# A two-layer diffusion-transformer step on one core: splits of the next weights at fixed chunks and the next rows scaled ahead, in the second half of the in-projection's first quarter

## The chip, the cores and the metric

The kernel runs on one core of one Trainium2 chip. The metric is the device time of one execution in microseconds (us). The core has five engines that run side by side: TensorE (PE: matmuls; PEld: its weight loads), VectorE (DVE), ScalarE (ACT), GpSimd (POOL), and SyncE (SP), whose queue issues the DMAs. Each engine takes its instructions in order and waits on semaphores for what others must finish first.

## The reference, cut to what matters

Two groups of 128 tokens (a context pass and a denoising step) go through two layers with the same weights. Each layer modulates its normalised input with scale, shift and gate vectors that are themselves products of a condition vector with a large matrix, `w_ada`; the first thing that layer 0 does with the result is the in-projection.

```python
def rmsnorm(x, g):
    xf = x.astype(jnp.float32)
    y = xf * lax.rsqrt(jnp.mean(xf * xf, axis=-1, keepdims=True) + EPS)
    return (y * g.astype(jnp.float32)).astype(x.dtype)
...
        mod = jax.nn.silu(cond) @ w_ada[l] + b_ada[l]
        sh1, sc1, gt1, sh2, sc2, gt2 = jnp.split(mod[:, None, :], 6, axis=-1)
        h = rmsnorm(x, g_norm_mix[l]) * (1 + sc1) + sh1
...
    proj = h @ w_in
```

The inner size is D = 2048, that is 16 blocks of 128, called rows here; the in-projection has 23 output blocks of 128, called chunks. All inputs are fp32.

## The kernel before, in words

**A product in three.** Every fp32 product is made of three matmuls at reduced precision. An operand is split into a high part (a rounding to `F32R`) and a low part (what the rounding left). For each 128x128 block of weights, `gemm` issues high weights by high rows, high weights by low rows, and low weights by high rows. The weights arrive by DMA as raw tiles of 16 blocks (1 MB, three buffers, `raw`); `split` makes the high part `wh` on ScalarE (L245) and the low part `wl` on VectorE (L246), each in tiles of 8 blocks with four buffers. The rows live in `hx`: for row c, the high part stands in columns 0 to 255 and the low part in 256 to 511.

**The in-projection in quarters.** Since the shift and scale vectors of layer 0 must first be computed from `w_ada`, the in-projection does not wait for all of them: it runs over the 23 chunks several times, each time with only some of the 16 rows, and adds up (`part`). First with rows 0 and 1 (weights `whole`, copied out of PSUM by ScalarE), then with rows 2 and 3 (weights `halves`, added on VectorE, L1132), then with rows 4 to 7, 8 to 11 and 12 to 15 (weights `rest`). A chunk with two rows is 6 matmuls, one with four is 12. The three accumulator banks (`pacc`) are taken in turn, so a chunk waits for the sum of the third chunk before it.

**The steps between the chunks.** In each pass, steps written out by hand stand after certain chunks: `first_half`, `other_half` and, for the later passes, `quarter(q)` are tables from chunk number to step, which `part` calls through `between(c)`. A *unit* is a quarter of one of the vectors: unit (0, 1, 1) is the scale of rows 4 to 7, unit (0, 0, 1) their shift. `pair(u, t)` sums two tiles of `w_ada` for unit u on TensorE (`ada<-araw,condw`, `ada<-kv_in,condw`); after the second pair ScalarE copies the sum (`am`, L437). `turned` lets TensorE transpose that copy (L110) and VectorE reduce it and add the bias (L453, L455; for a scale also L462). `turned(1)` then calls `rows(1)`, which is `modulate`: for rows 4 to 7 VectorE multiplies x with the row factor `rb0` (L648) and with scale and shift for the first group of tokens (L654), ScalarE does so for the second (L657) and rounds to the high part (L658), and VectorE and GpSimd in turn make the low part (L643).

`scaled_rows` and `begin_row` do the same work in two steps, and are used for rows 0 to 3 before: the first makes x times factor times scale (L669, L672, VectorE), which needs no shift; the second adds the shift and splits: the high part on ScalarE (L681), the low part on VectorE (L682).

**Order.** The instructions that pass through `keep_order`, and all of TensorE's while `pe.in_turn` is set, stay in the order written. The others, the splits in `Weights.chunk` among them, are placed by a scheduler before the run, on each engine where they fit by its own reckoning. `Weights.ahead` splits half a raw tile at a fixed place (`pin`), in pieces of `FINE` = 4 blocks. `Feed` issues the loads of `w_ada` tiles and raw weights in one order, each as soon as its buffer is free; `feed.use` gives a buffer back.

The table that is changed reads, before:

```python
                other_half = {5: lambda: pair(2, 2), 7: turned, 13: lambda: pair(3, 0), 20: lambda: pair(3, 2),
                              22: lambda: turned(1)}
```

Of the kernel before, what the change touches and what calls it, by code (L numbers as in the profile page):

```python
# [12 lines left out]
AF = mybir.ActivationFunctionType  # L13
ALU = mybir.AluOpType
# [3 lines left out]
P = 128  # L18
# [43 lines left out]
FINE = 4  # L62
# [29 lines left out]
def step_kernel(ctx: ExitStack, tc: tile.TileContext, A: dict):  # L92
    nc = tc.nc
    dve, act, pool, sp = nc.vector, nc.scalar, nc.gpsimd, nc.sync
    kept = []

    def keep_order(i):
        if not any(i is j for j in kept):
            kept[:] = [i]
            tc.keep_in_program_order(i)  # L100
# [37 lines left out]
    def T_(pl, shape, tag, dt=F32, bufs=None):  # L138
        kw = {} if bufs is None else {"bufs": bufs}
        return pl.tile(shape, dt, tag=tag, name=nm(tag), **kw)  # L140
# [95 lines left out]
    def spread(r, bank=bank):  # L236

        ps = bank()
        for g in range(2):
            pe.matmul(ps[:, g * T:(g + 1) * T], r[:, g:g + 1].to_broadcast([P, P]), ident, start=True, stop=True)  # L240
        return ps[:, :NT]


    def split(out_hi, out_lo, src, pin=lambda i: i):
        pin(act.copy(out_hi, src))  # L245
        pin(dve.tensor_tensor(out=out_lo, in0=src, in1=out_hi.bitcast(F32), op=ALU.subtract))  # L246
# [3 lines left out]
    class Weights:  # L250
# [30 lines left out]
        def ahead(self, pin, mid=None):  # L281

            if not self.half:
                self.half = [self.take()[0], 0]
            raw, lo = self.half
            self.blocks += self.halves(raw, lo, pin, mid)
            self.half = None if lo else [raw, 8]
            if lo:
                self.used()

        def halves(self, raw, lo, pin=lambda i: i, mid=None):
            wh = T_(wpool, [P, 1024], "wh", F32R, bufs=4)
            wl = T_(wpool, [P, 1024], "wl", F32R, bufs=4)
            for at in range(0, 8, FINE):
                s = slice(at * P, (at + FINE) * P)
                split(wh[:, s], wl[:, s], raw[:, (lo + at) * P:(lo + at + FINE) * P], pin)
                if mid and at == 0:
                    mid()
            return [(wh[:, b * P:(b + 1) * P], wl[:, b * P:(b + 1) * P]) for b in range(8)]

        def chunk(self):
            while len(self.blocks) < self.nblk:
# [362 lines left out]
    def scaled_rows(rb, c0, n):  # L665
        nts = []
        for c in range(c0, c0 + n):
            h = T_(tmp, [P, NT], "nt", bufs=4)
            keep_order(dve.tensor_tensor(out=h, in0=x[:, c], in1=rb, op=ALU.mult))  # L669
            for g in range(2):  # L670
                s = slice(g * T, (g + 1) * T)
                keep_order(dve.tensor_scalar(out=h[:, s], in0=h[:, s], scalar1=scl[:, 0, 0, c, g:g + 1],  # L672
                                             scalar2=None, op0=ALU.mult))
            nts.append(h)
        return nts

    def begin_row(hx, h, c):
        for g in range(2):
            s = slice(g * T, (g + 1) * T)
            b_ = mod[:, 0, 0, c, g:g + 1]  # L680
            keep_order(act.activation(hx[:, c, s], h[:, s], AF.Identity, bias=b_))  # L681
            keep_order(dve.scalar_tensor_tensor(  # L682
                out=hx[:, c, NT + g * T:NT + (g + 1) * T], in0=h[:, s], scalar=b_,
                in1=hx[:, c, s].bitcast(F32), op0=ALU.add, op1=ALU.subtract))
# [40 lines left out]
    def operand(pl, tag):  # L725
        return home(pl, tag)[:, :KD * ROW].rearrange("p (k n) -> p k n", k=KD)
# [181 lines left out]
    def mixer_ab(hx, beside):  # L908
        l = 0
        with tc.tile_pool(name="ab", bufs=1) as ab:  # L910
            with tc.tile_pool(name="abp", bufs=1) as pj:
# [53 lines left out]
                def unit_pair(u, t):  # L965
                    for i in (t, t + 1):
                        sum_rows(i, feed.tiles.pop((*u, i)))
                    for i in (t, t + 1):
                        feed.use(("a", "s1", "a", "s3")[i])

                whole = Weights(A["w_in_ab"][0:3], 2, 8, cycle=23)
                halves = Weights(A["w_in_ab"][3:6], 2, 8, cycle=23)
                rest = Weights(A["w_in_ab"][6:], 4, 4, cycle=23)
                for w in (whole, halves, rest):
                    w.used = lambda: feed.use("raw")
# [15 lines left out]
                weights(whole)  # L991
                units(2, (0, 1))
                weights(halves)
                units(2, (2, 3))
                weights(halves)
                units(3, (0, 1))
                weights(halves)
# [26 lines left out]
                rb0 = spread(r)  # L1024
# [6 lines left out]
                def first_rows():  # L1031
                    unit.copy()
                    unit.turn()
                    for c in range(2):
                        begin_row(hx, nts[c], c)
# [103 lines left out]
                def rows(q):  # L1139
                    modulate(hx, rb0, 0, 0, range(4 * q, 4 * q + 4))  # L1140

                second = {}

                def half_begin(j):
                    second["u"] = HalfUnit(j, 1, ppool["first"], att_bank)
                    for t in range(2):
                        half_sums(second["u"], t)
                    second["u"].copy()

                def half_end(j):  # L1150
                    second["u"].turn()
                    if j == 0:
                        for i, h in enumerate(second["nt"]):
                            begin_row(hx, h, 2 + i)
# [4 lines left out]
                def pair(u, t):  # L1159
                    unit_pair(ROWS[u], t)  # L1160
                    if t == 2:
                        second["finish"] = ada_finish(*ROWS[u], False)
                        second["finish"].pop(0)()

                def turned(q=0):
                    second["finish"].pop(0)()
                    if q:
                        rows(q)

                first_half = {0: lambda: whole.ahead(keep_order), 4: lambda: half_begin(1), 6: lambda: half_end(1),  # L1170
                              10: stretch, 13: lambda: half_begin(0), 15: lambda: half_end(0), 22: lambda: pair(2, 0)}
                other_half = {5: lambda: pair(2, 2), 7: turned, 13: lambda: pair(3, 0), 20: lambda: pair(3, 2),
                              22: lambda: turned(1)}

                def quarter(q):
                    u = 2 * q + 2
# [345 lines left out]
    with banks("pab") as ppool["ada"]:  # L1522
        ppool["att"] = ppool["ada"]
        idle = T_(tmp, [P, 512], "am", bufs=1)
        keep_order(dve.memset(idle, 0.0))
        ps = T_(pacc, [P, 512], "acc")
        for _ in range(WARM):
            keep_order(pe.matmul(ps, idle[:, :P], idle, start=True, stop=True))
        for c in range(0, KD, 4):
            keep_order(sp.dma_start(out=x[:, c:c + 4], in_=A["xT"][:, c:c + 4]))  # L1530
        ppool["first"] = lambda: T_(ppool["ada"], [P, 512], "ada", bufs=1)
        hx = operand(keep, "hx")
        st = stat_init()
        with tc.tile_pool(name="beside", bufs=1) as beside:
            o = mixer_ab(hx, beside)
            with tc.tile_pool(name="raw", bufs=1) as rp:
                T_(rp, [P, SHIFT // 4], "pad")
                u = raw_tile(rp, "u")
                out_ab(o, st, u)
                W = Weights(A["w_up"][0], KD, 1)  # L1540
                hx, *begun = modulated(st, 0, 1, W, u, (keep, "hx"), rp)
# [22 lines left out]
    for c in range(KD):  # L1564
        if c in EARLY:
            pool.tensor_tensor(out=x[:, c], in0=x[:, c], in1=rbs, op=ALU.mult)
        else:
            dve.scalar_tensor_tensor(out=x[:, c], in0=x[:, c], scalar=C("gfin")[:, c:c + 1], in1=rb,  # L1568
                                     op0=ALU.mult, op1=ALU.mult)
# [136 lines left out]
```

## Time and profile before

| | |
|---|---|
| median of 3 runs | 2341.16 us (2339.91 to 2343.24) |
| the profiled execution, its own time | 2337.55 us |
| its span in the profile | 2335.8 us |
| TensorE busy, share of the span | 2304.0 us, 99% |
| VectorE, ScalarE, GpSimd busy | 1853.1, 1192.0, 179.7 us |
| moved by DMA | 612.98 MB, 262 GB/s in the mean |

The pass with rows 2 and 3 runs from about 50 to 75 us of the span; rows 4 to 7 begin after it. Busy times overlap, since the engines work side by side, and TensorE's is modelled: matmuls follow each other in a pipeline, so the distance from one start to the next says more than a length. In an answer in order of time the columns are start, length, engine, line, operation, output<-input, shapes, count, and in brackets the idle time ahead with what ended it. L107 is the line of every matmul, L110 of every transpose.

### The profile page before, as it was taken

The numbers are of one execution on the slowest core, as the hardware profiler recorded it, in microseconds if no ns is written. First come the engines' busy times: TensorE is split into PE (matmuls) and PEld (weight loads), VectorE is DVE, ScalarE is ACT, GpSimd is POOL, SyncE is SP. The second block draws the span as 40 slices with busy tenths as digits, with TensorE's granted clock in tenths as the row PEclk, the third lists the DMA queues.
The fourth block names the chain that finished last, engine by engine and source line by source line (L and its number), as shares of the span: only waits on it lengthen the run. The fifth ranks groups of instructions, "written<-read, shape, count | busy, mean of one in ns | idle before, by whom it ended". The sixth has DMA issues, their size and how long they took to land.

```text
span 2335.8 us, 47901 instructions
## 1 busy us (share of the span) xinstructions
PE 2304.0 (99%) x19692; PEld 2192.2 (94%) x19692; DVE 1853.1 (79%) x2864; ACT 1192.0 (51%) x1969; POOL 179.7 (8%) x240
## 2 busy tenths in 40 slices
PE   8899999999999999999999999999999999999998
PEld 6788768999999999999999999999999999999998
DVE  4669768889999999999978888798899755666654
ACT  4345545665554355555564544457655434555543
POOL 0001111310000000001130000023000000000011
PEclk9999999999999999999999999999999999999999
DMA  9887779677767777777778788677677555555553
GB/s 387 349 349 289 294 286 358 231 281 270 269 246 297 289 269 259 267 271 253 289 268 292 284 312 295 251 286 269 236 259 266 197 198 188 194 198 197 187 195 127
DMA packets 107099, 612.98 MB, mean 262 GB/s; under 512 B 11584, under 2 KB 19712, under 8 KB 39296
## 3 DMA queue, kind: packets, MB, share of 16 engines
q1 hardware_dynamic: 106880, 609.92, 70.9%
q8 instruction: 155, 2.54, 0.4%
q14 instruction: 64, 0.52, 0.1%
HBM read 605.12 MB, written 4.75 MB: 261 GB/s over the span
## 4 chain that ended last, share of the span: by engine, by line
PE 95%; DMA 2%; DVE 2%; ACT 1%; issue 0%; SPq 0%; POOL 0%; DVEq 0%; ACTq 0%; POOLq 0%
PE acc L107 87%; PE ada L107 4%; PE att L107 2%; DMA araw<-w_ada 1%; PE att L110 1%; DMA raw<-w_in_ab 1%; DVE wl L246 1%; PE misc L107 1%; PE ada L110 0%; DMA block<-w_ada 0%; DVE aacc L510 0%; ACT wh L245 0%; DVE x L1568 0%; SPq L956 0%; PE misc L110 0%
## 5 line engine op out<-in xcount | busy, mean ns | idle before, releaser
L107 PE MATMUL acc<-hx,wh 128*128 128x256 f32 (+1 forms) x7296 | 1261.4, 278 | 8.7 <-DVE hx L643 3.6
L245 ACT CAST wh<-raw 128x1024 fp32r<-128x1024 f32 (+2 forms) x824 | 796.3, 976 | 917.7 <-PE acc L107 777.2
L246 DVE TENSOR_TENSOR wl<-raw,wh 128x1024 fp32r<-128x1024 f32 (+2 forms) x824 | 920.0, 1132 | 280.4 <-ACT wh L245 275.3
L107 PEld LDWEIGHTS acc<-hx,wh 128*128 128x128 f32 x7296 | 1103.8, 188 | 31.8 <-issue 11.7
L107 PE MATMUL acc<-hx,wl 128*128 128x256 f32 (+1 forms) x3648 | 1010.3, 277 | 2.8 <-DVE wl L246 2.8
L107 PEld LDWEIGHTS acc<-hx,wl 128*128 128x128 f32 x3648 | 686.5, 188 | 4.5 <-DVE wl L246 3.6
L107 PE MATMUL acc<-g,wh 128*128 128x256 f32 x2816 | 478.9, 276 | 0.0
L107 PEld LDWEIGHTS acc<-g,wh 128*128 128x128 f32 x2816 | 423.7, 188 | 0.0
L107 PE MATMUL acc<-g,wl 128*128 128x256 f32 x1408 | 388.2, 276 | 0.0
L107 PE MATMUL acc<-hxc,wh 128*128 128x256 f32 (+1 forms) x1536 | 277.4, 282 | 0.0
L481 DVE CUSTOM_DVE_ANT_0 junk<-araw,condb 128x2048 f32<-128x2048 f32 x120 | 275.7, 2298 | 0.0
L107 PEld LDWEIGHTS acc<-g,wl 128*128 128x128 f32 x1408 | 264.2, 188 | 0.0
L107 PEld LDWEIGHTS acc<-hxc,wh 128*128 128x128 f32 x1536 | 236.3, 188 | 8.7 <-issue 8.4
L107 PE MATMUL acc<-hxc,wl 128*128 128x256 f32 (+1 forms) x768 | 213.8, 278 | 0.0
L510 DVE SCALAR_TENSOR_TENSOR aacc<-block,condw,aacc 128x512 f32<-128x512 f32 x240 | 171.8, 754 | 28.4 <-DMA block<-w_ada 28.1
L208 POOL TENSOR_TENSOR sqacc<-sqacc,sq 128x256 f32<-128x256 f32 x62 | 72.0, 1161 | 1514.1 <-ACT sq L204 1508.0
L107 PEld LDWEIGHTS acc<-hxc,wl 128*128 128x128 f32 x768 | 144.7, 188 | 0.3
L1461 ACT ACTIVATE cv<-acc,convw 128x256 f32<-128x256 f32 x170 | 94.9, 559 | 0.0
L107 PE MATMUL ada<-araw,condw 128*32 128x512 f32 (+1 forms) x704 | 89.6, 592 | 3.0 <-DMA araw<-w_ada 3.0
L838 DVE SCALAR_TENSOR_TENSOR x<-acc,mod,x 128x128 f32<-128x128 f32 x190 | 57.3, 342 | 34.6 <-PE acc L107 34.5
L1467 DVE SCALAR_TENSOR_TENSOR cv<-acc,convw,cv 128x254 f32<-128x254 f32 x170 | 81.3, 478 | 3.3
L1464 DVE SCALAR_TENSOR_TENSOR cv<-acc,convw,cv 128x254 f32<-128x254 f32 x170 | 80.6, 474 | 0.0
(250 smaller groups left out, 1414.2 us busy)
## 6 DMA issues: line engine op xcount, KB each, us to landing
raw<-w_up SPq DMA_DIRECT2D x176, 1024.0 KB, 4.8
araw<-w_ada SPq DMA_DIRECT2D x144, 1024.0 KB, 5.7
raw<-w_down SPq DMA_DIRECT2D x88, 1024.0 KB, 4.8
raw<-w_in_c SPq DMA_DIRECT2D x48, 1024.0 KB, 5.9
block<-w_ada SPq DMA_DIRECT2D x128, 256.0 KB, 5.7
raw<-w_in_ab SPq DMA_DIRECT2D x18, 1024.0 KB, 9.8
raw<-w_out_ab SPq DMA_DIRECT2D x16, 1024.0 KB, 8.6
raw<-w_out_c SPq DMA_DIRECT2D x16, 1024.0 KB, 6.8
```

Of the source, the lines that this page charges most:

```text
L107: return self.placed(nc.tensor.matmul(*a, **kw))
L110: return self.placed(nc.tensor.transpose(*a, **kw))
L208: eng.tensor_tensor(out=st["acc"], in0=st["acc"], in1=sq, op=ALU.add)
L245: pin(act.copy(out_hi, src))
L246: pin(dve.tensor_tensor(out=out_lo, in0=src, in1=out_hi.bitcast(F32), op=ALU.subtract))
L481: keep_order(dve.tensor_tensor_reduce(out=T_(feat["pool"], [P, D], "junk"), in1=feat["row"][:, c], in0=feat["raw"].rearrange("p g n -> p ( ...
L510: i = dve.scalar_tensor_tensor(out=acc[c], in0=block, scalar=condw[:, k, c:c + 1], in1=acc[c], op0=ALU.mult, op1=ALU.add)
L838: dve.scalar_tensor_tensor(out=x[:, c, s], in0=ps[:, s], scalar=mod[:, l, 3 * which + 2, c, g:g + 1], in1=x[:, c, s], op0=ALU.mult, op1=AL ...
L1461: pin(act.activation(y, ps, AF.Identity, scale=cw[:, 1, m:m + 1], bias=cw[:, 3, m:m + 1]))
L1464: pin(dve.scalar_tensor_tensor(out=y3[:, :, 1:], in0=p3[:, :, :T - 1], scalar=cw[:, 0, m:m + 1], in1=y3[:, :, 1:], op0=ALU.mult, op1=ALU.add))
L1467: pin(dve.scalar_tensor_tensor(out=y3[:, :, :T - 1], in0=p3[:, :, 1:], scalar=cw[:, 2, m:m + 1], in1=y3[:, :, :T - 1], op0=ALU.mult, op1=A ...
```

## The change

Three things change in the pass with rows 2 and 3. The splits of raw tiles, those of `halves` and of the first tile of `rest`, are put at fixed places (after chunks 7, 8, 14, 15, 18 and 20), half a tile each, in pieces of four blocks; before, the scheduler placed them, mostly in pieces of eight. For that `ahead` and `halves` learn to take a tile that is not full. Rows 4 to 7 are made by `scaled_rows` after chunk 10 and `begin_row` after chunk 19 in place of `modulate` after chunk 22; for rows 5 and 7 the high part of the second group of tokens is made on VectorE (`both=False`), and GpSimd has no part in these rows. The pairs of unit (0, 0, 1) move from after chunks 13 and 20 to after 12 and 17, its turn from after 22 to after 19.

```diff
         def ahead(self, pin, mid=None):
 
             if not self.half:
-                self.half = [self.take()[0], 0]
-            raw, lo = self.half
-            self.blocks += self.halves(raw, lo, pin, mid)
-            self.half = None if lo else [raw, 8]
+                self.half = [*self.take(), 0]
+            raw, n, lo = self.half
+            self.blocks += self.halves(raw, lo, pin, mid, min(8, n - lo))
+            self.half = None if lo else [raw, n, 8]
             if lo:
                 self.used()
 
-        def halves(self, raw, lo, pin=lambda i: i, mid=None):
+        def halves(self, raw, lo, pin=lambda i: i, mid=None, n=8):
             wh = T_(wpool, [P, 1024], "wh", F32R, bufs=4)
             wl = T_(wpool, [P, 1024], "wl", F32R, bufs=4)
-            for at in range(0, 8, FINE):
-                s = slice(at * P, (at + FINE) * P)
-                split(wh[:, s], wl[:, s], raw[:, (lo + at) * P:(lo + at + FINE) * P], pin)
+            for at in range(0, n, FINE):
+                s = slice(at * P, min(at + FINE, n) * P)
+                split(wh[:, s], wl[:, s], raw[:, (lo + at) * P:min(lo + at + FINE, lo + n) * P], pin)
                 if mid and at == 0:
                     mid()
-            return [(wh[:, b * P:(b + 1) * P], wl[:, b * P:(b + 1) * P]) for b in range(8)]
+            return [(wh[:, b * P:(b + 1) * P], wl[:, b * P:(b + 1) * P]) for b in range(n)]
...
-    def begin_row(hx, h, c):
+    def begin_row(hx, h, c, both=True):
         for g in range(2):
             s = slice(g * T, (g + 1) * T)
             b_ = mod[:, 0, 0, c, g:g + 1]
-            keep_order(act.activation(hx[:, c, s], h[:, s], AF.Identity, bias=b_))
+            if g == 0 or both:
+                keep_order(act.activation(hx[:, c, s], h[:, s], AF.Identity, bias=b_))
+            else:
+                keep_order(dve.tensor_scalar(out=hx[:, c, s], in0=h[:, s], scalar1=b_, scalar2=None, op0=ALU.add))
             keep_order(dve.scalar_tensor_tensor(
...
-                other_half = {5: lambda: pair(2, 2), 7: turned, 13: lambda: pair(3, 0), 20: lambda: pair(3, 2),
-                              22: lambda: turned(1)}
+                def split_next(w):
+                    w.ahead(keep_order)
+
+                def four_scaled():
+                    second["nt"] = scaled_rows(rb0, 4, 4)
+
+                def four_rows():
+                    turned()
+                    for i, h in enumerate(second["nt"]):
+                        begin_row(hx, h, 4 + i, i % 2 == 0)
+
+                other_half = {5: lambda: pair(2, 2), 7: lambda: (turned(), split_next(halves)),
+                              8: lambda: split_next(halves), 10: four_scaled, 12: lambda: pair(3, 0),
+                              14: lambda: split_next(halves), 15: lambda: split_next(halves),
+                              17: lambda: pair(3, 2), 18: lambda: split_next(rest), 19: four_rows,
+                              20: lambda: split_next(rest)}
```

## The prediction

> **What bounds the kernel now.** I read the page's head first, then the busy times by stretch over the opening 200 us, then the order of instructions in time on TensorE and VectorE around the edit. The page gives the span and says that TensorE is the bound of the whole:
>
> ```profile
> span 2335.8 us, 47901 instructions
> PE 2304.0 (99%) x19692; PEld 2192.2 (94%) x19692; DVE 1853.1 (79%) x2864; ACT 1192.0 (51%) x1969; POOL 179.7 (8%) x240
> ```
>
> So an edit pays only where TensorE stands still or runs at a lower clock. The stretches show where that is; the columns are the stretch, its length, busy time (count) by engine, granted clock, DMA share, GB/s:
>
> ```profile
> 54.00:84.30 30.30, 22.51 (x174) 16.59 (x172) 20.18 (x41) 11.42 (x18) 3.40 (x2) 0.90 1.01 421
> 122.00:163.00 41.00, 41.00 (x350) 34.66 (x349) 26.94 (x51) 16.43 (x24) 1.64 (x2) 1.00 0.87 345
> 75.40:84.20 8.80, 2.82 (x13) 2.00 (x11) 8.35 (x16) 5.81 (x12) 3.40 (x2) 0.65 1.01 420
> 84.20:88.00 3.80, 3.71 (x17) 3.71 (x18) 1.12 (x4) 0.00 (x0) 0.00 (x0) 0.50 0.42 172
> ```
>
> The second half of the in-projection ends at 75.4 us. The next 8.8 us hold 2.82 us of matmuls and 8.35 us of VectorE work, and the 3.8 us after that run at a clock of 0.50. By 122 us there is no idle left. TensorE's own lines for this place (start, length, and in brackets the idle time and what ended it):
>
> ```profile
> 59.96 0.38 PE L107 MATMUL acc<-hx,wl 128*128 128x256 f32 x1 [0.98 <-DVE wl L246]
> 68.63 0.39 PE L107 MATMUL acc<-hx,wl 128*128 128x256 f32 x1 [0.74 <-DVE wl L246]
> 74.33 0.40 PE L107 MATMUL acc<-hx,wh 128*128 128x256 f32 x2
> 74.68 0.40 PE L107 MATMUL acc<-hx,wh 128*128 128x256 f32 x2
> 75.39 0.60 PE L110 MATMUL ada<-cst,am 128*128 128x128 f32 x4
> 78.45 0.58 PE L107 MATMUL acc<-hx,wh 128*128 128x256 f32 x1 [2.46 <-ACT hx L658]
> 80.11 0.58 PE L107 MATMUL acc<-hx,wh 128*128 128x256 f32 x1 [1.07 <-DVE hx L643]
> 84.29 0.58 PE L107 MATMUL acc<-hx,wh 128*128 128x256 f32 x1 [2.53 <-DVE hx L643]
> 84.89 0.63 PE L107 MATMUL acc<-hx,wh 128*128 128x256 f32 x2
> 85.53 0.63 PE L107 MATMUL acc<-hx,wh 128*128 128x256 f32 x2
> 88.08 0.46 PE L107 MATMUL acc<-hx,wh 128*128 128x256 f32 x2
> ```
>
> Three matmuls take 0.35 us at full clock (74.33 to 74.68), 0.117 each, and 0.64 us after the idle stretch (84.89 to 85.53), 0.213 each. Full pace is back at 88.08, with 24 matmuls of the next quarter done: 7 before 84.29 and 17 after it (the count of the 3.8 us stretch). At full clock 24 would take 2.8 us from the transposes' end near 75.8, that is until 78.6. So 88.1 - 78.6 = 9.5 us is the most that the turn of this unit can ever give back, 0.4% of the run. What ended the last wait is VectorE. Its queue through that stretch:
>
> ```profile
> 76.03 0.19 DVE L453 TENSOR_REDUCE mod<-ada 128x8 f32<-128x32 f32 x1
> 76.25 0.17 DVE L455 TENSOR_TENSOR mod<-mod,cst 128x8 f32<-128x8 f32 x1
> 76.34 1.22 DVE L246 TENSOR_TENSOR wl<-raw,wh 128x1024 fp32r<-128x1024 f32 x1
> 77.48 1.11 DVE L654 TENSOR_SCALAR nt<-nt,scl,mod 128x128 f32<-128x128 f32 x4
> 78.50 1.22 DVE L246 TENSOR_TENSOR wl<-raw,wh 128x1024 fp32r<-128x1024 f32 x1
> 79.64 0.42 DVE L643 TENSOR_TENSOR hx<-nt,hx 128x256 fp32r<-128x256 f32 x1
> 81.03 2.88 DVE L246 TENSOR_TENSOR wl<-raw,wh 128x1024 fp32r<-128x1024 f32 x2
> 83.83 0.41 DVE L643 TENSOR_TENSOR hx<-nt,hx 128x256 fp32r<-128x256 f32 x1
> 84.16 0.74 DVE L648 TENSOR_TENSOR nt<-x,misc 128x256 f32<-128x256 f32 x2
> ```
>
> The shift lands (76.03), four rows are made, and four weight remainders (wl, L246) stand between them, although only the first is needed at once. From the reduce to the last row's low part it is 84.24 - 76.03 = 8.2 us, nearly all of it VectorE at work.
>
> **The splits.** The number of elements split is the same; a split of 1024 becomes two of 512. One piece costs VectorE 0.68 busy, and the wide one overlaps its successor by 1.22 - (77.48 - 76.34) = 0.08; so 0.60 for a piece, 1.14 for the wide one. Two pieces cost 0.06 more than one wide split, ten pieces or so 0.3 in all, beside matmuls except where they are named below.
>
> ```profile
> L246 DVE TENSOR_TENSOR wl<-raw,wh 128x512 fp32r<-128x512 f32 x4 | 2.7, 683 | 0.0
> L682 DVE SCALAR_TENSOR_TENSOR hx<-nt,mod,hx 128x128 fp32r<-128x128 f32 x4 | 1.3, 349 | 0.5 <-ACT hx L681 0.5
> L672 DVE TENSOR_SCALAR nt<-nt,scl 128x128 f32<-128x128 f32 x4 | 1.0, 282 | 0.0
> L681 ACT ACTIVATE hx<-nt,mod 128x128 fp32r<-128x128 f32 x4 | 1.3, 394 | 0.0
> 64.23 1.85 PE ada L107 x16
> ```
>
> At chunk 7 the split now stands behind the unit's three small VectorE steps (0.31 for the first two, by 76.03 to 76.34, and 0.2 for the third), but its first piece is shorter by 0.54. Chunk 8's wait of 0.98 therefore stays as it is. At chunk 16 the wait of 0.74 ended with a wide split; with a piece it ends 0.4 earlier. I take 0.4.
>
> **The scaled rows** at chunk 10: per row one product of 0.33 and two of 0.20 (0.282 less the overlap), 2.9 us for four. VectorE has room for them: 20.18 us busy in the 30.3 us stretch, and a pair of 1.85 us on TensorE follows at chunk 12. If that cover were missing, an accumulator would come free late, 0.4 us at most by the order of the queue. I take nothing.
>
> **The pairs** move from chunks 13 and 20 to 12 and 17, past no other load on SP's queue; only the moment changes at which two buffers come free. The second pair needs its last tile:
>
> ```profile
> 56.76 0.64 SPq L942 DMA_DIRECT2D kv_in<-w_ada  x1
> kv_in<-w_ada SPq DMA_DIRECT2D x1, 1024.0 KB, 10.6
> 57.46 4.04 SPq L271 DMA_DIRECT2D raw<-w_in_ab  x2
> raw<-w_in_ab SPq DMA_DIRECT2D x1, 1024.0 KB, 11.2
> ```
>
> It is issued at 56.76 and lands 10.6 later, at 67.4. TensorE reaches the end of chunk 17 near 69.6 (the 72.9 of the next part, less two chunks and a pair): covered by 2 us. The two weight tiles with which the next quarter begins are issued at 57.5 and 61.2, and the second lands 11.2 later, at 72.4: ahead of the splits that chunk 18 now asks for and of those behind them. The DMA engines are full in this stretch (1.01), so an earlier issue brings nothing sooner.
>
> **The turn at chunk 19.** Three chunks of 0.70 fewer stand ahead of it, and 0.4 was saved: the transposes come at 75.39 - 2.1 - 0.4 = 72.9 rather than 75.39, so the reduce, 0.64 behind them as now (76.03), comes at 73.5. The built program's VectorE queue from there on, in order, is: reduce and bias (0.31); a piece, an add of chunk 20, a piece, an add of 21; two low parts; an add of 22; a low part and a high part of row 5; a row product for the quarter after; two pieces; four low parts; a high part of row 7; a wide remainder of the second tile, a row product, another wide remainder, a row product; and only then the low part of row 7's second half, which the twelve matmuls of the next quarter's first chunk need. The wide remainders belong to chunks 4 to 7, yet stand ahead. The sum: 0.31 + 4 x 0.60 + 2 x 1.14 + three adds and three products of 128x256 at 0.33 (83.83 to 84.16) = 2.0 + eight low parts at 0.27 (0.349 less 0.08) = 2.2 + two high parts at 0.20 = 0.4: together 9.6 us. ScalarE's six high parts (0.32 apart, 2 us) and its splits run beside this. So the last row is ready at 73.5 + 9.6 = 83.1 against 84.24. The turn begins 2.5 us earlier, but VectorE has 1.4 us more to do before the last row, since the adds of three chunks and the low parts that GpSimd used to make now stand in this queue. Left: 1.1 us. TensorE then has 10 matmuls behind it (all nine of the first three rows and one of the fourth), not 7: 3 x 0.117 = 0.35 more. As the gaps are nearly as long as before, I take it that the cold 3.8 us follow the resumption again.
>
> **The rest.** From 163 to about 360 us, where the queues are not written out by hand, the scheduler places instructions anew; beyond that the order is the same. TensorE is without gaps there but for one place, the last heads:
>
> ```profile
> 331.70 0.30 PE L110 MATMUL att<-cst,p 128*128 128x128 f32 x1 [1.25 <-DVE p L895]
> 333.50 1.26 PE L107 MATMUL att<-pT,vm 128*128 128x128 f32 x6 [0.62 <-ACT pT L879]
> 334.70:338.40 3.70, 3.70 (x26) 1.30 (x26) 1.05 (x5) 1.63 (x6) 0.06 (x1) 0.64 0.00 0
> 331.84 0.82 PE L107 MATMUL att<-kg,qb 128*128 128x128 f32 x4
> 336.33 0.35 DVE L896 TENSOR_SCALAR p<-p,rec 128x256 f32<-128x256 f32 x1
> ```
>
> That place costs 1.25 + 0.62 + 0.36 x 3.7 = 3.2 us now. In the new order more output-projection matmuls stand ahead of the first of these waits, but the transposes of the next head then follow almost directly on its scores, and scores to weights takes 4.0 us (332.66 to 336.68). One gap closes, another opens; bounds: -3.2 (all gone) and +4.0 + 0.36 x 3.7 = +5.3 (a whole softmax uncovered, then cold). Lacking a row nearer to one, I take 0.
>
> **Sum.** 1.1 + 0.35 = 1.5 us off, within 0.5 and 2.5 for the size of VectorE's sum. The profiled execution took 2337.55 us, 1.75 more than its span, and lies 3.6 below the median of the three runs, 2341.16; I take the difference off the median: 2339.7 us, 0.06% faster. That is less than 0.2% (4.7 us), about what a measurement of this kernel can tell from no change.
>
> **Clock: a rule weighed.** In this trace the clock is down at the latest by 80.11, where single matmuls take 0.58, and full again 3.8 us after 84.29. The Trainium skill, TensorE: Matmul & The Clock Gate, Part 1, says that the clock drops after an idle window of about 3.4 us and returns after as long a busy one. The trace agrees on the return and not quite on the drop: no idle bracket above exceeds 2.53. By the rule taken at its word the changed kernel, whose longest gap is near 3.1, might stay at full clock.
>
> **Rivals.** (1) The clock does not drop, since TensorE's work from 75 to 83 is more spread out (10 matmuls for 7). Then 17 matmuls go at 0.117 instead of 0.213, 1.6 us more: 2338.1. Against it: sparse bursts did not keep it up before. (2) The rows are not late: if the last low part were to come before the wide remainders, 3.0 us (two at 1.14, two products at 0.33) would leave the wait, and with the last heads' 3.2 us gone too: 2339.7 - 6.2 = 2333.5. For the first the built order speaks against it; both at once are unlikely. (3) Slower: the new order in the last heads leaves a softmax uncovered on top of what is there, the +5.3 of above, after the 1.5 gained: 2345.0; with the gain at its lower bound 2346. It decides if fewer than about 30 matmuls (4.0 / 0.117) stand between scores and transposes. For it: the built order shows them close together. Against it: a part of today's gap goes. (4) The change does nothing measurable at all, because the wait is VectorE's total work and that stays: 2341.2, inside the forecast's range.
>
> **How the numbers follow.** Forecast with (4) 0.50, (1) 0.12, (2) 0.18, (3) 0.20. Range 2333.5 to 2345.5: from (2) to (3), leaving out their farther halves. Its own range for the forecast is 2338.5 to 2341.5. Faster by over 0.2% (below 2336.5) takes (2) and a little of (1): 0.22; slower by over 0.2% (above 2345.8) takes most of (3): 0.18; within: 0.60.
>
> **What the profile after would show.** Right: the reduce near 73.5; a TensorE wait that ends near 83.1 with a low part (the new row of begin_row) as its releaser; two wide remainders just ahead of it on VectorE; a clock of about 0.5 for the next 3.8 us; the pair at chunk 17 without a wait on DMA. Wrong: TensorE resuming before 80 us, or later than 85; a second wait on the accumulator's adds between 62 and 70; idle of over 3 us between 163 and 360 us.

## The result, and the profile after

The changed kernel takes 2343.55 us (2340.73 to 2348.99, 20 runs), the kernel before 2340.01 us beside it (2335.68 to 2345.61, 20 runs): 1.0016 of its time, 95% interval 1.0009 to 1.0023. It is 3.5 us slower, where 1.5 us faster was forecast. The profiled execution took 2343.07 us with a span of 2341.2 us.

The page's head after, and the busy times by stretch (stretch, its length, busy time and count by engine, granted clock, DMA share, GB/s):

```profile
span 2341.2 us, 47918 instructions
PE 2308.7 (99%) x19692; PEld 2194.9 (94%) x19692; DVE 1856.2 (79%) x2882; ACT 1192.8 (51%) x1973; POOL 177.2 (8%) x238
```

```profile
54.00:84.30 30.30, 24.58 (x190) 18.45 (x188) 23.95 (x65) 11.04 (x22) 0.00 (x0) 0.94 1.01 421
122.00:163.00 41.00, 41.00 (x350) 34.66 (x350) 26.78 (x51) 16.48 (x23) 1.64 (x2) 1.00 0.88 349
75.40:84.20 8.80, 4.58 (x28) 3.71 (x26) 8.77 (x22) 4.79 (x10) 0.00 (x0) 0.81 1.01 419
85.00:91.00 6.00, 6.00 (x28) 6.00 (x29) 2.52 (x5) 1.04 (x1) 0.00 (x0) 0.50 0.45 186
```

VectorE has 3.8 us more to do between 54 and 84 us (23.95 against 20.18), GpSimd nothing. The granted clock is 0.50 through all six microseconds of the last row; the row of the kernel before with that clock is 3.8 us long.

TensorE around the turn, in order of time:

```profile
61.58 0.38 PE L107 MATMUL acc<-hx,wl 128*128 128x256 f32 x1 [1.05 <-DVE wl L246]
70.00 0.38 PE L107 MATMUL acc<-hx,wl 128*128 128x256 f32 x1 [0.25 <-DVE wl L246]
78.20 0.38 PE L107 MATMUL acc<-hx,wh 128*128 128x256 f32 x1 [0.71 <-DVE hx L685]
79.09 0.36 PE L107 MATMUL acc<-hx,wh 128*128 128x256 f32 x1 [0.38 <-DVE hx L684]
80.79 0.52 PE L107 MATMUL acc<-hx,wh 128*128 128x256 f32 x1 [1.35 <-DVE hx L685]
84.97 0.58 PE L107 MATMUL acc<-hx,wh 128*128 128x256 f32 x1 [2.55 <-DVE hx L685]
90.69 0.60 PE L107 MATMUL acc<-hx,wh 128*128 128x256 f32 x2
91.25 0.41 PE L107 MATMUL acc<-hx,wh 128*128 128x256 f32 x2
```

VectorE's queue behind the reduce, cut to what decides:

```profile
75.36 0.19 DVE L453 TENSOR_REDUCE mod<-ada 128x8 f32<-128x32 f32 x1
...
80.39 1.14 DVE L685 SCALAR_TENSOR_TENSOR hx<-nt,mod,hx 128x128 fp32r<-128x128 f32 x4
81.44 0.28 DVE L684 TENSOR_SCALAR hx<-nt,mod 128x128 fp32r<-128x128 f32 x1
81.64 1.22 DVE L246 TENSOR_TENSOR wl<-raw,wh 128x1024 fp32r<-128x1024 f32 x1
82.77 0.41 DVE L648 TENSOR_TENSOR nt<-x,misc 128x256 f32<-128x256 f32 x1
83.10 1.22 DVE L246 TENSOR_TENSOR wl<-raw,wh 128x1024 fp32r<-128x1024 f32 x1
84.24 0.41 DVE L648 TENSOR_TENSOR nt<-x,misc 128x256 f32<-128x256 f32 x1
84.57 0.35 DVE L685 SCALAR_TENSOR_TENSOR hx<-nt,mod,hx 128x128 fp32r<-128x128 f32 x1
```

The last wait is again for a low part made by VectorE, now that of row 7, and the two wide remainders stand just ahead of it. (In the kernel before it was that of row 6: seven products, two rows and one more, were done ahead of it, and GpSimd made the low parts of rows 5 and 7.) The other place that changed is the end of the heads. After:

```profile
335.12 0.94 PE L107 MATMUL att<-pT,vm 128*128 128x128 f32 x6 [0.62 <-ACT pT L882]
337.45 0.30 PE L110 MATMUL att<-cst,p 128*128 128x128 f32 x1 [1.40 <-DVE p L898]
348.30 1.06 PE L107 MATMUL ada<-araw,condw 128*32 128x512 f32 x8 [2.18 <-DMA araw<-w_ada]
387.21 0.60 PE L110 MATMUL ada<-cst,am 128*128 128x128 f32 x4
```

The third row is new: an `ada` pair waits 2.18 us for its tile. To see how much is lost where, take marks that both programs reach with the same work behind them, each a row of transposes (`ada<-cst,am`) or the product that waits 0.62 us for ScalarE. Before, they stand at 58.15, 104.75, 162.84, 333.50 and at the row below; after, at 59.70, 106.16, 164.17, 335.12 and 387.21:

```profile
382.32 0.60 PE L110 MATMUL ada<-cst,am 128*128 128x128 f32 x4
```

| stretch, up to the mark | before | after | difference |
|---|---|---|---|
| first transposes of the second half | 58.15 | 59.70 | +1.55 |
| next quarter's first transposes (the turn lies between) | 46.60 | 46.46 | -0.14 |
| last turn of the in-projection | 58.09 | 58.01 | -0.08 |
| sixth head's second product | 170.66 | 170.95 | +0.29 |
| transposes behind the heads | 48.82 | 52.09 | +3.27 |
| end of the span | 1953.48 | 1953.99 | +0.51 |

The 1.55 us of the opening vary from one execution to the next: in a second execution of the same changed kernel (`after_again`, below) the first transposes come at 58.35, and in the twelve runs below between 57.96 and 59.37. What is left is one place, the last 50 us around the heads' end, which the edit doesn't touch in the source. There TensorE stands idle for 0.37 us of the 48.82 before and for 4.07 us of the 52.09 after. The turn itself is worth 0.1 us.

### The profile page after: what moved, and what is told of

It is laid out like the page before. It is cut to its first block, busy times and chain, and to the rows that moved or that the text cites. A ratio compares the mean times of both kernels' runs of the same rounds, so it can differ in the third digit from the quotient of the medians.

```text
span 2341.2 us, 47918 instructions
## 1 busy us (share of the span) xinstructions
PE 2308.7 (99%) x19692; PEld 2194.9 (94%) x19692; DVE 1856.2 (79%) x2882; ACT 1192.8 (51%) x1973; POOL 177.2 (8%) x238
## 4 chain that ended last, share of the span: by engine, by line
PE 94%; DMA 2%; DVE 2%; ACT 1%; issue 0%; POOL 0%; SPq 0%; DVEq 0%; ACTq 0%
PE acc L107 86%; PE ada L107 4%; PE att L107 2%; DMA araw<-w_ada 1%; DMA block<-w_ada 1%; PE att L110 1%; PE misc L107 1%; DVE wl L246 1%; DVE aacc L510 1%; PE ada L110 0%; ACT wh L245 0%; ACT p L873 0%; DVE x L1585 0%; DVE ql L1052 0%; PE misc L110 0%
## 5 line engine op out<-in xcount | busy, mean ns | idle before, releaser
L245 ACT CAST wh<-raw 128x1024 fp32r<-128x1024 f32 (+1 forms) x830 | 796.9, 971 | 913.5 <-PE acc L107 770.5
L246 DVE TENSOR_TENSOR wl<-raw,wh 128x1024 fp32r<-128x1024 f32 (+1 forms) x830 | 921.4, 1126 | 276.9 <-ACT wh L245 271.6
## 6 DMA issues: line engine op xcount, KB each, us to landing
block<-w_ada SPq DMA_DIRECT2D x128, 256.0 KB, 6.0
```

## The experiments

Theory 1: the scheduler's new order of the later instructions costs the time, and the turn gains little. Theory 2: the edit itself costs, and the later stages only shift. From the last quarter's pass to the end of the heads both kernels issue the same 1744 instructions, so an order can be written in: a list of places per engine, and a chain that holds each instruction behind its forerunner in the queue, without a wait.

```diff
+                mark = len(nc.cur_bb.bb.instructions)
                 pe.in_turn = False
                 pinned[0] = True
...
                 flush()
+                hold(mark)          # for b, a in zip(order, order[1:]): a queues behind b
```

**Orders exchanged.** The old second half with the new later order, the new second half with the old later order, and the changed kernel once more beside them.

> The kernel before, with its own second half, but from the last quarter's pass to the end of the heads every engine's instructions stand in the order that the scheduler gave them in the changed kernel. Theory 1 (the later order is the loss; the edit itself is worth a little): about 3.9 us over the kernel before, 2344 us, and the lost time arises between 170 and 366 us, with the wait of the ada pair for its DMA near 348 us. Theory 2 (the edit itself costs, what comes later only shifts): within 1 us of the kernel before, 2340 us.

> The changed kernel with its new second half, but from the last quarter's pass to the end of the heads every engine's instructions stand in the order of the kernel before. Theory 1: 0.2 to 1.5 us under the kernel before, 2338.5 to 2339.8 us (the turn's gain as one execution showed it, and as it was forecast). Theory 2: as slow as the changed kernel, 2343.5 us.

> The changed kernel once more, beside the two with exchanged orders. Both theories: 3.5 us over the kernel before, 2343.5 us. Theory 1: last product of the heads with a wait of about 2 us on the ada pair's DMA again; the slow stretch after the turn may last between 3.8 and 6.2 us, since it lasted so long in one execution each. Theory 2: it lasts 6.2 us again, as something that the edit brings.

Kernel before in these runs: 2339.89 us. The kernel before with the new order takes 2344.56 us (ratio 1.0023, 1.0014 to 1.0032); the changed kernel with the old order 2339.58 us (0.9998, 0.9989 to 1.0006); the changed kernel again 2343.32 us (1.0015, 1.0007 to 1.0024). The loss goes with the order and not with the edit. The kernel before in the new order shows the same rows as the changed kernel (in the kernels with an order written in, line numbers are higher by 50 to 70):

```profile
336.06 0.30 PE L162 MATMUL att<-cst,p 128*128 128x128 f32 x1 [1.41 <-DVE p L959]
346.91 1.52 PE L159 MATMUL ada<-araw,condw 128*32 128x512 f32 x8 [2.19 <-DMA araw<-w_ada]
387.66 0.60 PE L162 MATMUL ada<-cst,am 128*128 128x128 f32 x4
```

The changed kernel in the old order lacks them, and is through at 381.27 us:

```profile
83.72 0.58 PE L160 MATMUL acc<-hx,wh 128*128 128x256 f32 x1 [2.53 <-DVE hx L750]
104.70 0.60 PE L163 MATMUL ada<-cst,am 128*128 128x128 f32 x4
381.27 0.60 PE L163 MATMUL ada<-cst,am 128*128 128x128 f32 x4
```

The changed kernel once more: resumption at the same moment, the same wait on the DMA.

```profile
83.62 0.58 PE L107 MATMUL acc<-hx,wh 128*128 128x256 f32 x1 [2.53 <-DVE hx L685]
346.71 1.06 PE L107 MATMUL ada<-araw,condw 128*32 128x512 f32 x8 [2.25 <-DMA araw<-w_ada]
```

**Where in the new order.** The two orders have exactly the same instructions behind them at one point, 332.5 us: 958 of TensorE's 1043. Either order was taken up to there, and the other behind it.

> The kernel before; from the last quarter's pass its engines keep their own order up to the transposes of the sixth head's second product (332.5 us, where both orders have the same instructions behind them), and the rest of the heads, 85 instructions of TensorE and what belongs to them, stands in the changed kernel's order. Theory 1 (the whole loss of the new order lies behind 332.5 us, in how the last heads' softmaxes, the ada pairs and the output products stand): as before_new_order, 4 to 5 us over the kernel before, 2344 to 2345 us. Theory 2 (it is spread over the heads): half of it or less, 2342.5 us or less.

> The reverse: the kernel before with the changed kernel's order up to 332.5 us, and its own order behind it. Theory 1: within 1 us of the kernel before, 2339 to 2341 us. Theory 2: 2 us over it or more, 2342 us.

Kernel before: 2339.47 us. Old up to 332.5 us and new behind it: 2346.19 us (1.0023, 1.0014 to 1.0032), all of the loss. New first and old behind: 2341.21 us (1.0005, 0.9996 to 1.0014), not told apart from none, though the interval leaves room for up to 3.3 us; its profile puts the part ahead of 332.5 us at 170.98 us against 170.66, and at the seam it has waits of its own. Both, in that order:

```profile
349.47 1.06 PE L160 MATMUL ada<-araw,condw 128*32 128x512 f32 x8 [2.25 <-DMA araw<-w_ada]
390.17 0.60 PE L163 MATMUL ada<-cst,am 128*128 128x128 f32 x4
```

```profile
336.24 1.30 PE L159 MATMUL misc<-aacc,cst 128*32 128x256 f32 x6 [1.57 <-DVE aacc L574]
350.23 0.30 PE L162 MATMUL att<-cst,p 128*128 128x128 f32 x1 [0.70 <-DVE p L959]
```

So 85 instructions of TensorE, and what belongs to them on the other engines, carry the loss. From the sixth head's second product to the transposes behind the heads the old order takes 47.6 to 48.8 us in seven executions, the new one 52.1 to 55.3 in four, that with the old order ahead of it among them. Left out are the kernel with the new order first (51.1), the one that moves a part (55.4) and `rows_first_free` below: there the scheduler itself gives the engines the old sequence again, and it takes 50.3 us with a wait of 1.51 us for a weight remainder in it.

**One wait in it.** In the old order the sixteen products of two `ada` tiles fill the gap at 335 us; in the new one they start at 341 to 342, the loads that need their two buffers are issued about 4 us later (341.95 in the kernel before with the new order, 337.56 in the kernel before), and the next tile lands late. The kernel before, then the changed kernel:

```profile
335.55 2.83 PE L107 MATMUL ada<-araw,condw 128*32 128x512 f32 x16
342.25 1.90 PE L107 MATMUL ada<-araw,condw 128*32 128x512 f32 x16
```

Moved forward:

> The kernel before with the changed kernel's later order (as in before_new_order), and in it one thing moved on TensorE: the side bank's 4 sums and the 16 products of two ada tiles stand ahead of the transpose that waits 1.41 us for the softmax at 336.06, instead of at 340.39. Theory 1 (the new order loses because that pair frees its two araw buffers 5 us later, so that the next ada tile lands late: 2.19 us of wait and about 1.5 us of products at half pace behind it): 3.7 to 5.1 us under before_new_order, 2339.5 to 2341 us, no DMA wait near 347 us. Theory 2 (the new order loses in many small places): 1.5 us under it or less, 2343 us or more.

2345.71 us, against 2340.33 of the kernel before (1.0022, 1.0012 to 1.0032): nothing gained. The wait on the DMA is down to 0.2 us, and two others are there:

```profile
338.24 1.30 PE L159 MATMUL misc<-aacc,cst 128*32 128x256 f32 x6 [2.56 <-DVE aacc L574]
...
352.04 0.48 PE L162 MATMUL att<-cst,p 128*128 128x128 f32 x1 [2.26 <-DVE p L959]
```

The side bank's sums, which must stand ahead of the pair, were not ready on VectorE in that order, and the last softmax was late behind them. That the late buffers alone are the cause was expected and is not borne out. Whether they are one of several causes this run can't say, since the move brought a wait of its own.

**The two halves of the edit**, each alone, with the old later order:

```diff
 splits_only:  {5: pair(2, 2), 7: (turned, split_next(halves)), 8: split_next(halves), 13: pair(3, 0), 14, 15: split_next(halves),
                18: split_next(rest), 20: (pair(3, 2), split_next(rest)), 22: turned(1)}
 rows_only:    {5: pair(2, 2), 7: turned, 10: four_scaled, 12: pair(3, 0), 17: pair(3, 2), 19: four_rows}
```

> The fixed splits of the next weights (chunks 7, 8, 14, 15, 18, 20) alone; unit, rows and their chunks as in the kernel before (pairs at 13 and 20, turned at 22), later order of before. Theory 1 (VectorE's queue between the reduce and the last row's low part sets the resume; the splits change little in it): within 0.7 us of the kernel before, 2339.2 to 2340.6 us. Theory 2 (the two halves of the edit work against each other, the splits losing what the rows gain): 1.5 to 3 us over the kernel before.

> The rows scaled ahead at chunk 10, pairs at 12 and 17 and the unit turned at chunk 19 alone; the next weights split where the scheduler puts it, later order of before. Theory 1: the same 4.9 us of splits stand in VectorE's queue behind the reduce as in the changed kernel, so the resume comes within 0.6 us of after_old_order's, and the time within 1 us of it, 2338.6 to 2340.6 us. Theory 2: 1.5 to 3 us under the kernel before, 2337 to 2338.4 us.

2339.79 us (0.9998, 0.9989 to 1.0006) and 2340.01 us (0.9999, 0.9990 to 1.0007): neither moves the time, as theory 1 had it. Underneath, theory 1 had expected the splits to change little, and they change more: alone they bring the rows sooner (resumption at 82.78, the next quarter's transposes 45.0 us after the first ones, against 46.1 to 46.6 in five executions of the old second half), and then TensorE waits at the turn into the last quarter:

```profile
82.78 0.58 PE L160 MATMUL acc<-hx,wh 128*128 128x256 f32 x1 [1.19 <-DVE hx L708]
167.58 0.39 PE L160 MATMUL acc<-hx,wh 128*128 128x256 f32 x1 [1.02 <-DVE hx L708]
```

**VectorE's queue.** If the two wide remainders ahead of row 7's last low part set the resumption, it must come sooner when they are split later:

```diff
+                    early = {0: lambda: split_next(rest), 1: lambda: split_next(rest)} if q == 1 else {}
-                    return {4: lambda: pair(u, 0), ...
+                    return {**early, 4: lambda: pair(u, 0), ...
```

> The changed kernel with the order of before from the last quarter's pass on, and the splits of the second tile of the next weights fixed at chunks 0 and 1 of the next pass, so that two wide remainders of 1.22 us each leave VectorE's queue ahead of the last row. Theory 1 (VectorE's queue sets the resume, as predicted): resume 2.4 us earlier after the reduce (7.1 instead of 9.56 us from reduce to the last row's low part); 2.4 us under the changed kernel with that order if the slow stretch of the clock stays, up to 5.5 us under it if the shorter pause leaves the clock up. Theory 2 (something else of the edit costs): resume as before within 0.5 us, because ScalarE's parts or the matmuls' own wait end last.

> The changed kernel with the second tile's splits fixed at chunks 0 and 1 of the next pass, as rows_first, but no order written in: the scheduler places what comes later, and puts the last heads as in the kernel before. Theory 1 (the turn's 2.4 us and more are kept, and the last heads decide the rest): as rows_first, 2335 to 2337 us. Theory 2 (the written order itself had given rows_first its time): 2338 us or more.

2335.85 us against 2339.89 (0.9987, 0.9978 to 0.9995); without an order written in 2336.57 against 2339.47 (0.9984, 0.9975 to 0.9993). From reduce to last low part 80.55 + 0.35 - 73.61 = 7.29 us, and the last wait shrinks from 2.53 to 0.26:

```profile
73.61 0.19 DVE L518 TENSOR_REDUCE mod<-ada 128x8 f32<-128x32 f32 x1
80.55 0.35 DVE L750 SCALAR_TENSOR_TENSOR hx<-nt,mod,hx 128x128 fp32r<-128x128 f32 x1
80.95 0.58 PE L160 MATMUL acc<-hx,wh 128*128 128x256 f32 x1 [0.26 <-DVE hx L750]
85.39 0.49 PE L160 MATMUL acc<-hx,wh 128*128 128x256 f32 x2
101.40 0.60 PE L163 MATMUL ada<-cst,am 128*128 128x128 f32 x4
```

From the first transposes to the next quarter's it is 43.44 us, 2.8 less than in the changed kernel with the old order (46.26). This is the version that beats both kernels, and with `rows_first_free` it needs nothing but the two lines above. The scheduler then keeps the old sequence in the last heads, the one that the changed kernel lost; one wait of 1.51 us for a weight remainder at 369 us stands in its profile.

**The clock.** In `rows_first` the products still run at half pace from 80.95 to 85.39, though TensorE stands still for only 0.26 us ahead of them. Extra products in the waits:

```diff
+    FILLS = {0: 5, 1: 11, 3: 8}       # behind the first product of block i, into a bank nobody reads
+    pe.matmul(junk[:, :NT], w, hx[:, 0, :NT], start=True, stop=True)
```

> rows_first with 24 extra products of 128x256 (0.113 us each at full pace) into a bank that nobody reads, in the waits of the first chunk of the next pass: 5, 11 and 8 behind the first product of its blocks 0, 1 and 3. Theory 1 (the slow stretch after the turn comes from the idle time in these waits, 1.9 to 2.6 us of 3.4 us; it is left only at the end of a stretch of 3.4 us without idle time): no slow products at 79 to 85 us, 1.6 to 3.2 us under rows_first, 2332.7 to 2334.2 us. Theory 2 (the slow stretch has another cause, such as the load of the other engines or the DMAs): slow products as before, and the fills cost up to 1 us, 2336 to 2337 us.

> rows_first_fill with the order of rows_first on VectorE, ScalarE, GpSimd and the DMA queue, so that the 24 extra products are the only difference to rows_first. Theory 1 (rows_first_fill lost the 1.9 us of its turn again because the scheduler put splits ahead of the next turn's rows: 0.76 and 1.45 us of wait at 122 and 124 us): no such waits, 1.6 to 2.2 us under rows_first, 2333.7 to 2334.3 us. Theory 2 (the next turn waits for VectorE as soon as TensorE is 2 us earlier, whatever the order): waits of 1.5 us or more there again, 2335.5 to 2338 us.

With the fills the clock stays up, 1.00 where `rows_first` has 0.69. First `rows_first`, then the fills in its order:

```profile
75.40:84.20 8.80, 6.11 (x28) 5.25 (x27) 7.54 (x22) 3.68 (x9) 0.00 (x0) 0.69 1.01 422
```

```profile
75.40:84.20 8.80, 8.19 (x63) 7.33 (x62) 8.46 (x25) 4.98 (x12) 0.00 (x0) 1.00 1.01 422
```

The turn takes 41.5 and 41.4 us instead of 43.4. In the first of the two kernels the scheduler had answered the fills by putting splits ahead of the following turn's rows, and TensorE waited there:

```profile
122.26 0.39 PE L163 MATMUL acc<-hx,wh 128*128 128x256 f32 x1 [0.76 <-ACT hx L726]
124.10 0.38 PE L163 MATMUL acc<-hx,wh 128*128 128x256 f32 x1 [1.45 <-DVE hx L711]
```

It took 2338.14 us against 2340.33 (0.9993, 0.9984 to 1.0002). With the order of `rows_first` these waits are gone, and up to 159 us the profile keeps 1.9 us, 1.3 up to 378; the time, 2336.05 us against 2339.47 (0.9981, 0.9972 to 0.9991), isn't told apart from that of `rows_first`. Theory 1's mechanism is shown at the turn; its 1.6 to 2.2 us in the time are not.

## Why the prediction was wrong

**The turn, step by step.** The reduce was put at 73.5 and came at 75.36, or 73.8 without the opening's 1.55 (74.11 and 74.02 in two more executions of the same second half). VectorE's sum from the reduce to the last row was put at 9.6 us: 84.57 + 0.35 - 75.36 = 9.56. Chunk 8's wait stayed (1.05), chunk 16's fell by about the 0.4 forecast (0.74 to 0.25), the pair at chunk 17 waited for no DMA, and the order with the two wide remainders is the one worked out. Counted from the first transposes, the resumption comes 25.27 us on instead of 26.14: 0.9 us sooner, for 1.1. All this held, and `rows_first` shows that the queue is the cause. One label in the working is wrong without changing the sum: the row that ends at 84.24 in the kernel before is row 6, not the last one.

**The first mis-sized term: the cold stretch.** The prediction let the same 3.8 us follow the resumption. Read off the granted clock, 3.9 us follow it in the kernel before (84.29 to 88.19) and 6.2 in the changed kernel (84.97 to 91.13); 2.9 to 3.9 us in five executions with the old second half, 5.3 to 6.2 in three with the new one. The step behind it was to count from the resumption: the slow stretch lasts 10.24 us in both profiles, counted from the moment at which the clock falls, and that lies 6.3 us ahead of the resumption in the one and 4.1 in the other (the last section has the figures). Some 2 us more at half pace lose about 1 us, and so the 1.2 us gained by the resumption and by three products done ahead of it come out as nothing: from the first transposes to the next quarter's 46.1 to 46.6 us in five executions of the old second half, 46.0 to 46.5 in three of the new. How much of this belongs to the edit and how much to the moment at which an execution meets the clock's windows was not tested.

**The step that failed: the rest, taken as 0.** The prediction had seen that the scheduler places anew what lies between 163 and 360 us, had named the last heads as the one place with gaps, and had bounds of -3.2 and +5.3; for want of a nearer row it took 0. It is +3.3 in the profile of the changed kernel, and 2344.56 - 2339.89 = 4.7 us when that order alone is put into the kernel before. The profile of the kernel before has 3.4 us at a clock of 0.50 in that place (333.95 to 337.36), that of the changed kernel none; against the changed kernel with the old order, which has none either, the stretch is 52.09 - 47.56 = 4.5 us longer. The place was that of the third rival (2345.0 us at a chance of 0.20), the wait was not: a softmax is late by 1.40 us, hardly more than the 1.25 before, and what comes on top is an `ada` tile that lands 2.18 us late. That its time comes near the measured 2343.55 is luck. Of the prediction's own signs of error one was met: over 3 us of idle between 163 and 360 us. The first two rivals fell: the clock was at 0.50 behind the turn, and TensorE waited 2.55 us for the last row. The fourth, that the edit does nothing at the turn, comes nearest there in its outcome, not in its reason: the rows did come sooner, and the clock took it back. One chance does not follow from its sum: 0.18 for above 2345.8 us rests on a rival that was put at 2345.0.

What stays open: which of the queues in the last heads must change for the new order to lose nothing. Only one move in it was tried, and it traded one wait for two.

## What to carry to other kernels

Where a scheduler places a part of the program, an edit far from that part can cost more there than it gains where it was made: cut the span at marks with the same work behind them, and hold the order of one part fixed to time the other. A gain at one turn is kept only if the next stage's queue is ready as much sooner; here fills at one turn came back as waits at the following one until that order was held. And in a queue that sets the end, look first at what stands in it and isn't needed yet: moving two remainders of 1.22 us in the changed kernel gave 3.7 us (2335.85 against 2339.58), more than the whole edit.

## What the runs showed of the hardware

Read in steps of 0.1 us, the granted clock is either 1.00 or 0.50, and the moments of change can be told to a few hundredths of a microsecond. Five of the fourteen profiled executions, at the turn:

| execution | clock falls | resumption | clock is back | slow for |
|---|---|---|---|---|
| kernel before | 77.95 | 84.29 | 88.19 | 10.24 us |
| changed kernel | 80.89 | 84.97 | 91.13 | 10.24 us |
| kernel before, new order | 81.14 | 84.52 | 87.96 | 6.83 us |
| `splits_only` | 78.94 | 82.78 | 85.77 | 6.83 us |
| `rows_first_free` | 79.77 | 81.07 | 86.60 | 6.83 us |

Of the other nine, three are slow for 10.24 us there, four for 6.83, and the two with fills not at all; nine more slow stretches, in the last heads, last 3.41 us each. So every slow stretch from 46 to 400 us lasts one, two or three times 3.41 us, and where an execution has several, their starts lie a whole number of these apart: 77.95 and 333.95 in the kernel before, 256.0 us or 75 of them. Against the work they shift from one execution to the next: the clock falls 21.2 us behind the first transposes in the changed kernel and 20.3 in `after_again`, which is the same kernel. The Trainium skill, TensorE: Matmul & The Clock Gate, Part 1, "What's actually happening", says that the hardware watches windows of about 3.4 us which run freely, and that the clock comes back after a busy one. The lengths and the starts agree with that.

In the kernel before with the new order the resumption at 84.52 stands just ahead of the second window, which begins at 84.55, and the clock is back at its end. In the changed kernel the second window begins at 84.31, the resumption comes 0.66 us into it, and a third window is paid for. Over all twelve slow stretches at the turn, the clock came back after windows with at most 0.48 us of waits and stayed down after windows with 0.55 us and more, with one exception: in `rows_first_free` it stayed down after a first window with waits of 0.28 us. On the way down the section asks for an idle window; here windows with 1.7 to 2.7 us of waits were enough, in pieces too (0.71, 0.38 and 1.35 us in the changed kernel), and at this turn windows with up to 1.5 us were not. What else than waiting time decides stays open, and no run varied the moment of the resumption alone.
